# Moving a skipped overflow block behind the last expert, with twelve constant matmuls in its old place

## The chip, the cores and the metric

The kernel runs on one core of one Trainium2 chip. The metric is device time in microseconds (us), from one execution of the whole program; the kernel before has a median of 1113.36 us over 3 runs (1112.92 to 1116.15).

## The reference

One residual layer over 1024 tokens of width 1024, all in float32, and a last norm. The mixer (a gated recurrence and a softmax attention) comes first and is not touched by the change. Then comes a mixture of experts in two levels:

```python
pg = softmax(t @ w_group + b_group)            # 4 groups, top 1
e_logits = (t @ w_expert + b_expert)[group]    # 4 experts in it, top 2
gates = one_hot(expert_id, 16) * weights       # each token goes to 2 of 16 experts
for e in range(16):
    h = silu(t @ w_gate[e]) * (t @ w_up[e])    # 1024 -> 512
    y = y + gates[:, e:e+1] * (h @ w_down[e])  # 512 -> 1024
h = h + y
out = rms_norm(h, final_norm)                  # h * rsqrt(mean(h*h) + 1e-6) * gain
```

## The kernel before, in words

The kernel is one long, unrolled program, written with a planner that assigns semaphores and buffers. The planner gives each engine its own list of instructions. An instruction that is written later may be issued earlier if its inputs and its buffer are ready; what is written earlier goes first where both are ready. `tc.issue_after(ins)` puts what is written inside its block, on the engine of `ins`, behind `ins` in that engine's list; it adds no wait for other engines.

After the mixer, the function `back(i)` routes tile `i` of 128 tokens (there are eight): norm, transposes, the router's matmul (L819), the choice of group and experts on VectorE, and the rank of each token within its expert by a matmul with a triangular constant (L836). `enlist(i)` scatters the token numbers and gates into a list per expert in HBM (`list_d`). Tokens stand normed in `t_d` and as residual `h_d`, both in HBM.

When all tiles are routed, the experts are sorted by their number of tokens. Each place in that order has a fixed capacity (192, 160, 136 or 128 tokens). If an expert got more tokens than its place holds, the rest goes into blocks of 128 "overflow" rows. Their number, `tov`, is computed on the chip, and `tvi` and `ordi` (L912, L914) hold it and the order; `last_v` is the VectorE instruction that writes `ordi`.

Then follow, in the order written: the gather of expert 0's tokens (L925 and L930, GpSimd's indirect DMA), the definitions of the expert functions, and the load of `tov` into a register of all five engines (L1151) with the overflow block under `tc.If(tov > 0)` (L1152 to L1204). The block builds a list of overflow rows, loops over the overflow blocks, loads the weights of each block's expert into buffers `WT[3..5]` and adds the result to `h_d`. Behind it, `ready` and the copy of L1206 hold back the split of the weights and the load of the fourth weight matrix, and the loop over 16 experts begins.

The first expert and most others use `expert_t`: transposes of the gathered tokens (L1057), split of each weight matrix into two parts `wh` and `wl` (L1045 on ScalarE, L1047 on VectorE or GpSimd), and three matmuls for each product (L246 to L248, `mm3`). The last two experts use `expert`, with plain float32 matmuls (L989, L1001, L1009). Six weight buffers `WT` of 2 MB hold two experts' weights; a load is issued by SyncE when its buffer is free.

While expert 14 runs, `final_all` reads all rows of `h_d` back, norms them and writes them to the output. Expert 14's rows (`final_rows`, L1289) and expert 15's rows (`final`, L1256) are normed by themselves and overwrite their rows of the output by GpSimd's indirect DMA. Before the change, `final` keeps expert 15's finished rows in a tile `y0`.

Of the kernel before, what the change touches and what calls it, by code (L numbers as in the profile page):

```python
# [7 lines left out]
F32 = mybir.dt.float32  # L8
F32R = mybir.dt.float32r
I32 = mybir.dt.int32  # L10
U32 = mybir.dt.uint32
AF = mybir.ActivationFunctionType
OP = mybir.AluOpType
AX = mybir.AxisListType
# [3 lines left out]
D = 1024  # L18
S = 1024
NT = S // 128  # L20
KD = D // 128
E = 16
# [5 lines left out]
NOV = 16  # L28
NSLOT = E * CAP
NROW = NSLOT + NOV * 128  # L30
EPS = 1e-6
NU = 16
NWARM = 14
BIG = 1.0e30
NEG = 3.0e38
LEVELS = (1, 2, 4, 8, 16, 32, 64)
# [44 lines left out]
def build(ctx, tc, x, attn_norm, w_in, hg_lb_logits, hg_norm, fox_f_bias, fox_norm, w_out, ffn_norm,  # L81
          w_group, b_group, w_expert, b_expert, w_gate, w_up, w_down, final_norm, cf, ci, cl0, out, dbg=None):
    nc = tc.nc
# [16 lines left out]
    def cbank():  # L100
        return ps.tile([128, 512], F32, name="ch", tag="ch", bufs=NB["ch"])
# [26 lines left out]
    def C(k):  # L128
        o, n = offs[k]
        return cft[:, o:o + n] if o < nce else cfl[:, o - nce:o - nce + n]  # L130
# [53 lines left out]
    b = rbank()  # L184
# [555 lines left out]
    NW = 6  # L740
# [147 lines left out]
    b = bank()  # L888
# [26 lines left out]
    with tc.tile_pool(name="me", bufs=2, side="right", reuse_waits="tile") as me:  # L915
# [45 lines left out]
        with tc.issue_after(gathered[-1].ins):  # L961
            enlist(NT - 1)
        ready = [None, None]
        fnc = me.tile([1, 1], F32, name="fnc", bufs=1)

        def xprep(rows, xg):
# [13 lines left out]
        def expert(W, rows, xT, last=None, mid=None, res=None):  # L980
# [15 lines left out]
            if last:  # L996
                (m, idx, gt), = rows
                by = (cbank(), cbank())
                for q in range(4):
                    for c in range(2):  # L1000
                        T.matmul(by[c][0:m], hT[:, q, 0:m], wd[:, q, c * 512:c * 512 + 512], start=q == 0, stop=q == 3)  # L1001
                final(me.tile([m, D], F32, name="y0", bufs=1), m, idx, [z[0:m] for z in by], gt, last[0])
                return
            yT = me.tile([128, KD, WCAP], F32, name="yT", bufs=1)
            for k0, k1 in ((0, 3), (3, 6), (6, 8)):
# [142 lines left out]
                                              in_=yr, in_offset=None, compute_op=OP.add)  # L1148
                tc.declare_no_dep(p1.ins, p0.ins, reason="distinct rows")

        tov = nc.values_load(tvi, min_val=0, max_val=NOV)  # L1151
        with tc.If(tov > 0):  # L1152
            olist = dr.tile([NOV * 128, 2], F32, name="olist")
            G.dma_start(olist, cl0[NSLOT:NSLOT + NOV * 128])
            dg = me.tile([E, 2, E], F32, name="dg", bufs=1)
            V.tensor_scalar(dg[:, 0], e16, qc[:, 5:6], None, op0=OP.mult)
            V.tensor_scalar(dg[:, 1], e16, qc[:, 3:4], None, op0=OP.mult)
            b = cbank()
            T.matmul(b[:, 0:2 * E], ones[0:E, :], dg.rearrange("e a b -> e (a b)"), start=True, stop=True)
            ntl = me.tile([128, 4, E], F32, name="ntl", bufs=1)  # L1160
            V.tensor_copy(ntl[:, 0], b[:, 0:E])
            V.tensor_copy(ntl[:, 3], b[:, E:2 * E])
            lt2 = me.tile([128, E, E], F32, name="lt2", tag="sg")
            V.tensor_mul(lt2, C(C_LT).rearrange("p (a b) -> p a b", a=E), ntl[:, None, 0].to_broadcast([128, E, E]))
            V.tensor_reduce(ntl[:, 1], lt2, axis=AX.X, op=OP.add)
            V.tensor_add(ntl[:, 2], ntl[:, 1], ntl[:, 0])
            V.tensor_tensor(lt2, ntl[:, None, 2].to_broadcast([128, NOV, E]), C(C_JJ)[:, :, None].to_broadcast([128, NOV, E]), op=OP.is_le)
            oi = me.tile([128, NOV], F32, name="oi", bufs=1)
            V.tensor_reduce(oi, lt2, axis=AX.X, op=OP.add)
            V.tensor_scalar(oi, oi, float(E - 1), None, op0=OP.min)  # L1170
            oii = me.tile([128, NOV], I32, name="oii", bufs=1)
            V.tensor_copy(oii, oi)
            t1 = me.tile([128, 2 * NT, E], F32, name="t1", tag="sg")
            cp = me.tile([128, 2, NT], F32, name="cp", bufs=1)
            V.tensor_mul(t1, e1a.rearrange("p c i e -> p (c i) e"), ntl[:, 3:4].to_broadcast([128, 2 * NT, E]))
            V.tensor_reduce(cp.rearrange("p c i -> p (c i)"), t1, axis=AX.X, op=OP.add)
            V.tensor_mul(t1, e1a.rearrange("p c i e -> p (c i) e"), ntl[:, 1:2].to_broadcast([128, 2 * NT, E]))
            od = me.tile([128, 2, 2, NT], F32, name="od", bufs=1)
            V.tensor_reduce(od[:, 0].rearrange("p c i -> p (c i)"), t1, axis=AX.X, op=OP.add)
            V.tensor_sub(cp, rks, cp)  # L1180
            V.scalar_tensor_tensor(od[:, 0], od[:, 0], 128.0, cp, op0=OP.mult, op1=OP.add)
            V.tensor_scalar(od[:, 1], cp, 0.0, 1.0e6, op0=OP.is_lt, op1=OP.mult)
            V.tensor_add(od[:, 1], od[:, 1], od[:, 0])
            oix = me.tile([128, 2, NT], I32, name="oix", bufs=1)
            V.tensor_copy(oix, od[:, 1])
            for i in range(NT):
                for c in range(2):
                    G.indirect_dma_start(
                        out=olist, out_offset=bass.IndirectOffsetOnAxis(ap=oix[:, c, i:i + 1], axis=0),
                        in_=tg[:, c, i], in_offset=None, bounds_check=NOV * 128 - 1, oob_is_err=False)  # L1190
            with tc.For_i(0, tov) as j:
                ev = nc.values_load(oii[0:1, bass.ds(j, 1)], min_val=0, max_val=E - 1)
                lj = me.tile([128, 2], F32, name="lj")
                nc.sync.dma_start(lj, olist[bass.ds(j * 128, 128), :])
                li = me.tile([128, 1], I32, name="li")
                V.tensor_copy(li, lj[:, 0:1])
                W = []
                for q, w_ in enumerate((w_gate, w_up, w_down)):
                    src = w_[0, bass.ds(ev, 1)].rearrange("a (k p) c -> p (a k) c", p=128)
                    t = WT[3 + q].rearrange("p (k c) -> p k c", c=src.shape[2])  # L1200
                    nc.sync.dma_start(t, src)
                    W.append(t)
                rows = [(128, li, lj[:, 1:2])]
                expert(W, rows, xprep(rows, gather(rows)))  # L1204
        ready[:] = [None, last_v]
        G.tensor_copy(WT[3][0:1, 0:1], xg[0][0:1, 0:1])  # L1206
        wload(3)
# [95 lines left out]
        for e in range(E):  # L1303
            last = None
            if e == E - 1:
                last = held(e)
            nx = xg1 if e == 0 else gather(rows_of(e + 1), part_of(e + 1)) if e + 1 < E else None
            W = [loaded.get(3 * e + q) for q in range(3)]
            if e == 0:
                expert_t(W, rows_of(e), xg, part=part_of(e), pre=pre)  # L1310
            else:
                ft = final_all() if e == E - 2 else None
                if e < E - 2 and (part_of(e) or len(rows_of(e)) == 1):
                    expert_t(W, rows_of(e), xg, part_of(e))
                else:
                    xT = xT if last else xprep(rows_of(e), xg)
                    xT = expert(W, rows_of(e), xT, last, ft, held(e) if ft else None)
            xg = nx
            for q in range(3):
                if 3 * e + NW + q < 3 * E:  # L1320
                    wload(3 * e + NW + q)
    we_cm.__exit__(None, None, None)
    ps_cm.__exit__(None, None, None)
    ho_cm.__exit__(None, None, None)
# [23 lines left out]
```

## Time and profile before

| | |
|---|---|
| median of 3 runs | 1113.36 us |
| profiled execution, whole | 1111.55 us |
| its span, first to last instruction | 1109.7 us |
| TensorE busy | 1044.7 us (94%) |
| VectorE, ScalarE, GpSimd busy | 672.3, 489.2, 363.3 us |
| mean granted TensorE clock | 0.971 of full speed |

The profile is of one execution. PE is the matmul side of TensorE and PEld its weight loads; DVE is VectorE, ACT ScalarE, POOL GpSimd, SP SyncE. A name with q is the engine's queue, whose waits, branches and loads into registers are not counted as busy. PEclk is the clock that was granted to TensorE; it has two levels, 0.50 (1.2 GHz) and 1.00 (2.4 GHz). The routing ends and the first expert begins between 700 and 722 us; the experts run until about 1095 us.

### The profile page before, as it was taken

How to read it: one execution, taken by the hardware profiler on the slowest of the kernel's cores; microseconds unless marked ns; L12 is line 12 of the kernel's file. 1: busy time of each engine (PE TensorE's matmuls, PEld its weight loads, DVE VectorE, ACT ScalarE, POOL GpSimd, SP SyncE). 2: the span in 40 equal slices, each digit the busy share in tenths (PEclk: the TensorE clock that was granted, in tenths of full speed). 3: DMA queues.
4: the chain of work that ended last, by engine and by line, in shares of the span. 5: the costliest groups of instructions: out<-in, count | busy, mean ns of one | idle time of the engine just before them, and what ended most of it. 6: DMA issues, size and time to landing. Idle time of an engine off the chain costs nothing. (4 is left out here: it accounts for less than half of the span.)

```text
span 1109.7 us, 19260 instructions
## 1 busy us (share of the span) xinstructions
PE 1044.7 (94%) x7471; PEld 886.3 (80%) x7471; DVE 672.3 (61%) x1600; ACT 489.2 (44%) x845; POOL 363.3 (33%) x283
## 2 busy tenths in 40 slices
PE   7999999999999998899989899699999999999994
PEld 6989878778989887789867788576877778878793
DVE  5436445663596338825564676666778778777445
ACT  6423232422444233414442233465666767667341
POOL 2024113221141114300321233354655556545312
PEclk8999999999999999999989999699999999999997
DMA  7120521224111521163316952369999999999974
GB/s 244 40 58 21 158 62 38 67 49 105 39 46 32 135 64 30 59 185 128 99 54 216 385 165 76 126 221 373 370 332 319 362 320 376 301 321 373 290 294 168
DMA packets 103007, 197.12 MB, mean 178 GB/s; under 512 B 9660, under 2 KB 43564, under 8 KB 102912
## 3 DMA queue, kind: packets, MB, share of 16 engines
q1 hardware_dynamic: 91616, 173.12, 45.0%
q0 software_dynamic: 7568, 20.96, 7.6%
q10 hardware_dynamic: 3728, 1.77, 0.6%
q8 instruction: 60, 0.98, 0.4%
q14 instruction: 35, 0.29, 0.1%
HBM read 155.85 MB, written 30.68 MB: 168 GB/s over the span
## 5 line engine op out<-in xcount | busy, mean ns | idle before, releaser
L246 PE MATMUL bk<-whi,xhi 128*128 128x256 f32 (+1 forms) x384 | 112.6, 293 | 4.0 <-ACT whi L176 2.0
L1047 DVE TENSOR_TENSOR wl<-we,wh 128x1024 fp32r<-128x1024 f32 x64 | 91.8, 1445 | 34.7 <-ACT wh L1045 33.9
L248 PE MATMUL bk<-whi,xlo 128*128 128x256 f32 (+1 forms) x384 | 111.4, 290 | 0.2 <-DVE xlo L213 0.2
L247 PE MATMUL bk<-wlo,xhi 128*128 128x256 f32 (+1 forms) x384 | 110.4, 288 | 1.1 <-DVE wlo L177 1.1
L247 PE MATMUL ch<-wl,xh 128*128 128x512 f32 (+1 forms) x336 | 108.7, 324 | 0.0
L1045 ACT CAST wh<-wm 128x1024 fp32r<-128x1024 f32 x84 | 87.2, 1049 | 48.3 <-PE ch L248 47.6
L248 PE MATMUL ch<-wh,xl 128*128 128x512 f32 (+1 forms) x336 | 107.7, 322 | 0.0
L246 PE MATMUL ch<-wh,xh 128*128 128x512 f32 (+1 forms) x336 | 107.7, 327 | 0.0
L246 PE MATMUL bk<-xhi,whi 128*128 128x512 f32 x256 | 104.0, 406 | 1.7 <-DVE kl L299 1.4
L1045 ACT CAST wh<-we 128x1024 fp32r<-128x1024 f32 x84 | 87.2, 1049 | 39.8 <-PE ch L248 39.6
L1047 DVE TENSOR_TENSOR wl<-wm,wh 128x1024 fp32r<-128x1024 f32 x63 | 93.1, 1507 | 17.1 <-ACT wh L1045 17.1
L248 PE MATMUL bk<-xhi,wlo 128*128 128x512 f32 x256 | 103.1, 403 | 0.0
L247 PE MATMUL bk<-xlo,whi 128*128 128x512 f32 x256 | 102.5, 400 | 0.0
L246 PEld LDWEIGHTS bk<-whi,xhi 128*128 128x128 f32 x384 | 73.8, 192 | 5.8 <-ACT whi L176 2.3
L387 ACT ACTIVATE Lg<-Lg,mn 128x128 f32<-128x128 f32 (+3 forms) x64 | 49.7, 777 | 60.9 <-DVE mn L383 54.3
L247 PEld LDWEIGHTS bk<-wlo,xhi 128*128 128x128 f32 x384 | 74.1, 193 | 1.9 <-DVE wlo L177 1.6
L248 PEld LDWEIGHTS bk<-whi,xlo 128*128 128x128 f32 x384 | 74.1, 193 | 0.8 <-DVE xlo L213 0.4
L1047 POOL TENSOR_TENSOR wl<-we,wh 128x1024 fp32r<-128x1024 f32 x20 | 51.1, 2554 | 70.9 <-ACT wh L1045 70.9
L521 POOL TENSOR_TENSOR hK<-hK,hF 128x512 f32<-128x512 f32 x28 | 36.6, 1306 | 108.5 <-PE hc L503 100.5
L177 DVE TENSOR_TENSOR wlo<-wraw,whi 128x1024 fp32r<-128x1024 f32 (+1 forms) x26 | 33.3, 1279 | 63.8 <-ACT whi L176 63.8
L247 PEld LDWEIGHTS ch<-wl,xh 128*128 128x128 f32 x336 | 64.3, 191 | 9.1 <-issue 4.1
L405 ACT CAST ph<-ch 128x512 fp32r<-128x512 f32 (+1 forms) x80 | 43.0, 542 | 64.5 <-PE ch L400 62.4
(419 smaller groups left out, 2645.8 us busy)
## 6 DMA issues: line engine op xcount, KB each, us to landing
we<-in_w_gate_dram SPq DMA_DIRECT2D x8, 2048.0 KB, 19.8
we<-in_w_up_dram SPq DMA_DIRECT2D x8, 2048.0 KB, 18.3
we<-in_w_down_dram SPq DMA_DIRECT2D x8, 2048.0 KB, 18.0
wm<-in_w_gate_dram SPq DMA_DIRECT2D x8, 2048.0 KB, 8.4
wm<-in_w_up_dram SPq DMA_DIRECT2D x8, 2048.0 KB, 13.5
wm<-in_w_down_dram SPq DMA_DIRECT2D x8, 2048.0 KB, 15.2
wraw<-in_w_in_dram SPq DMA_DIRECT2D x26, 512.0 KB, 3.9
xt<-in_x_dram SPq DMA_DIRECT2D x8, 512.0 KB, 13.8
```

The source lines that it names most:

```text
L177: V.tensor_sub(lo, raw, hi.bitcast(F32))
L246: T.matmul(o, l[0], r[0], start=first, stop=False)
L247: T.matmul(o, l[0], r[1], start=False, stop=False)
L248: T.matmul(o, l[1], r[0], start=False, stop=last)
L387: A.activation(L[:, :nb * 128], L[:, :nb * 128], AF.Exp, scale=-1.0, bias=prev, accum_out=fl[:, 0, i, hh:hh + 1])
L405: LF['act'] = A.copy(ph[:, :o], b[:, :o])
L521: G.tensor_mul(k2[:, :, 0], k2[:, :, 0], tb.to_broadcast([128, n, hs]))
L1045: A.copy(hi, src)
L1047: (G if j % 3 == 2 else V).tensor_sub(lo, src, hi.bitcast(F32))
```

## The change

Three edits. The `If` with the overflow block moves, with its body as it was, behind the loop over the experts. As the output's rows are then already written, its body first writes expert 15's rows into `h_d` (they were only kept on the chip) and, at its end, runs `final_all` again. `final` keeps those rows in weight buffer `WT[3]` instead of `y0`, and `yl` remembers them. The load of `tov` into the registers stands behind expert 1. Where the `If` stood, twelve float32 matmuls of a constant with itself (`ones`, 128x128) write a PSUM bank that nothing reads.

```diff
+NGAP = 12
...
+        yl = []
...
-                final(me.tile([m, D], F32, name="y0", bufs=1), m, idx, [z[0:m] for z in by], gt, last[0])
+                yl.append(WT[(3 * E - 3) % NW][0:m, 0:D])
+                final(yl[0], m, idx, [z[0:m] for z in by], gt, last[0])
...
-        tov = nc.values_load(tvi, min_val=0, max_val=NOV)
-        with tc.If(tov > 0):
-            olist = dr.tile([NOV * 128, 2], F32, name="olist")
...
+        b = cbank()
+        with tc.issue_after(last_v.ins):
+            for _ in range(NGAP):
+                T.matmul(b[:, 0:128], ones, ones, start=True, stop=True)
         ready[:] = [None, last_v]
         G.tensor_copy(WT[3][0:1, 0:1], xg[0][0:1, 0:1])
         wload(3)
...
         for e in range(E):
...
                     xT = expert(W, rows_of(e), xT, last, ft, held(e) if ft else None)
+                if e == 1:
+                    tov = nc.values_load(tvi, min_val=0, max_val=NOV)
             xg = nx
...
+        with tc.If(tov > 0):
+            (m, idx, _), = rows_of(E - 1)
+            G.indirect_dma_start(out=h_d, out_offset=bass.IndirectOffsetOnAxis(ap=idx, axis=0), in_=yl[0], in_offset=None)
+            olist = dr.tile([NOV * 128, 2], F32, name="olist")
...
+            fa = final_all()
+            next(fa)
+            next(fa)
```

## Rows read from the trace of the kernel before

**Rows 1.** The page: busy time of an engine, share, instructions.

```profile
PE 1044.7 (94%) x7471; PEld 886.3 (80%) x7471; DVE 672.3 (61%) x1600; ACT 489.2 (44%) x845; POOL 363.3 (33%) x283
```

**Rows 2.** Windows: start:end, length, busy by engine (instructions), clock, DMA, GB/s.

```profile
700.00:750.00 50.00, 39.37 (x275) 31.03 (x275) 31.49 (x93) 27.11 (x36) 22.97 (x18) 0.80 0.56 190
750.00:800.00 50.00, 49.59 (x276) 36.29 (x275) 34.80 (x37) 30.71 (x38) 24.75 (x15) 1.00 1.05 369
...
1000.00:1050.00 50.00, 49.59 (x366) 38.98 (x359) 32.20 (x35) 27.34 (x35) 25.76 (x15) 1.00 0.98 336
```

**Rows 3.** Waits, 730 to 1060 us: total us, times, longest; largest of TensorE.

```profile
PEld ch L246 <- issue: 4.9, 10, 0.8
```

**Rows 4.** Windows of 4 us from routing to the first expert.

```profile
702.00:706.00 4.00, 1.71 (x8) 1.58 (x8) 2.61 (x19) 2.84 (x6) 1.99 (x2) 0.50 0.36 134
...
718.00:722.00 4.00, 4.00 (x13) 3.23 (x12) 1.38 (x2) 1.33 (x3) 0.00 (x0) 0.50 0.73 231
722.00:726.00 4.00, 4.00 (x19) 3.06 (x17) 2.93 (x5) 2.85 (x4) 0.27 (x1) 0.98 0.79 301
```

**Rows 5.** Timeline, 700 to 722 us: start, length, instruction, idle time before it.

```profile
701.48 1.72 PE L819 MATMUL ch<-wrt,tT 128*128 128x24 f32 x8
...
705.49 3.88 ACT L1045 CAST wh<-we 128x1024 fp32r<-128x1024 f32 x4 [0.19 <-issue]
705.49 0.61 PE L836 MATMUL ch<-mem,cfl 128*128 128x16 f32 x2 [2.29 <-DVE mem L833]
...
709.71 1.00 POOL L925 DMA_INDIRECT xg<-t_d,i  x1 [5.42 <-DVE qc L904]
...
710.20 0.21 PE L910 MATMUL bk<-perm,cfl 16*1 16x16 f32 x2
...
711.02 1.67 POOL L930 DMA_INDIRECT xgr<-t_d,ri  x1 [0.30 <-DVE ordi L914]
...
716.39 1.94 PE L1057 MATMUL bk<-cft,xg 128*128 128x128 f32 x8 [5.99 <-PEq L1152]
...
717.56 0.18 POOL L1206 COPY wm<-xg 1x1 f32<-1x1 f32 x1 [2.23 <-PE bk L1057]
```

**Rows 6.** Source view of L1152: ns min/median/max, first and last start; who waited.

```profile
L1152 POOLq EVENT_SEMAPHORE  x5: 17/43/4052, 712.2 to 716.5; - x5
...
L1152 PEldq COMPARE_BRANCH  x1: 4707/4707/4707, 711.2 to 711.2; - x1
...
L1152 POOLq COMPARE_BRANCH  x1: 57/57/57, 711.7 to 711.7; - x1
L1152 POOLq INC_SWDGE_SEM  x1: 736/736/736, 716.6 to 716.6; - x1
...
  PE bk L1057: 6.0, 1
```

**Rows 7.** Source view of L1151, the load of `tov`, on TensorE's queue.

```profile
L1151 PEldq TENSOR_LOAD <-tvi x1: 492/492/492, 710.6 to 710.6; - x1
```

**Rows 8.** DMA view, 700 to 730 us: what, queue, count, us from issue to landing.

```profile
xg<-t_d,i POOLq DMA_INDIRECT x1, 4.4
xgr<-t_d,ri POOLq DMA_INDIRECT x1, 4.8
```

**Rows 9.** Timeline of TensorE: passes of 128x128 at the start and near the end.

```profile
1.08 5.43 PE L186 MATMUL rb<-warm 128*128 128x128 f32 x28 [1.08 <-DVE br_bc L217]
...
1079.07 8.65 PE L989 MATMUL ch<-xT,wm 128*128 128x128 f32 x76
```

**Rows 10.** Timeline of the end: the last instructions of ScalarE and GpSimd.

```profile
1097.65 0.72 ACT L1254 ACTIVATE we<-we,qz 128x512 f32<-128x512 f32 x1 [0.29 <-DVE qz L1253]
...
1101.24 1.00 POOL L1256 DMA_INDIRECT out_dram<-we,la  x1 [2.19 <-DMA out_dram<-we,la]
```

**Rows 11.** DMA view, 1070 to 1110 us: the scatters into the output.

```profile
out_dram<-we,la POOLq DMA_INDIRECT x3, 3.2
```

**Rows 12.** Source view of L1344, the program's end, on GpSimd's queue.

```profile
L1344 POOLq DRAIN  x1: 7850/7850/7850, 1101.0 to 1101.0; - x1
```

More of the change, by code (lines that the diff above doesn't have):

```diff
@@ L1149, in expert_t @@
                 tc.declare_no_dep(p1.ins, p0.ins, reason="distinct rows")
-        tov = nc.values_load(tvi, min_val=0, max_val=NOV)
-        with tc.If(tov > 0):
-            olist = dr.tile([NOV * 128, 2], F32, name="olist")
[L1154 to L1204, printed above, removed]
```

51 lines of the change are left out of this document (added).

## The prediction, made before the changed kernel ran

> **What bounds the kernel now.** I read the page first: its engine table and the stages of 50 us [rows 1, 2]. TensorE is busy for 94% of the span, and from 750 to 1050 us for 49.6 of every 50 us. The longest wait of one TensorE instruction there is 0.8 us [rows 3]. So in the experts TensorE is the bound, and time lost before the first expert is handed on to the end almost one for one; nothing later can absorb it. The stage 700 to 750 is the exception: 39.37 us busy and a granted clock of 0.80 [rows 2]. I therefore cut that stage into 4 us pieces [rows 4]: from 702 to 722 us the clock stands at 0.50 (1.2 GHz). The timeline [rows 5] names the work: the router's last matmuls (L819) end at 703.2, TensorE then waits 2.3 us for VectorE's ranking of the tokens (L836), works in small pieces until L910 ends at 710.41, and the first transposes of expert 0 (L1057) start at 716.39. The source view of L1152, the `If`, says why [rows 6]: TensorE's branch takes 4707 ns, and TensorE's wait ahead of L1057, 6.0 us, is put down to it. Last I read the end, where the change puts the `If`.
>
> **Start of the first expert.** Removed from this place: the load of `tov` (0.49 us on TensorE's queue [rows 7]), the branch, and on GpSimd a chain that ends with L1206 at 717.56. What is late next is the gather of the 128 tokens: it starts at 709.71 [rows 5] and lands 4.4 us later [rows 8], at 714.1. With 0.2 us for the wait, the transposes could start at 714.3, that is 2.1 us earlier; zero if the gather lands late, and no more than 2.3. The part rows `xgr` (issued 711.02, landing in 4.8 us, so 715.8 [rows 5, 8]) are read after those eight transposes, which take 1.94 us [rows 5], so they hide. SyncE's load of the fourth weight matrix is held by L1206 and comes up to 2 us sooner; none of TensorE's waits in the experts is for a weight DMA [rows 3], so I count it as nothing. If that cover went, the weight would be late for expert 1 only.
>
> **The twelve matmuls.** The 14 calls of L186, the same form, are 28 passes, so these are 24 of 128x128. L186 takes 5.43 us for its 28, or 0.194 us each, at the program's start; L989 at full clock takes 8.65 us for 76, 0.114 us each [rows 9]. That is 4.65 us or 2.7 us of TensorE. The code puts them in a block queued behind `last_v`, but `last_v` is a VectorE instruction and that call orders only instructions of the same engine; the matmuls read only a constant. So nothing ties them to this place, and the planner may issue them as soon as TensorE has nothing else ready. Rows 5 show it doing that to others: ScalarE's casts of L1045, written behind the `If`, run at 705.49, before it. Two bounds follow. If they stand behind L910, they run from 710.45 to 715.1 and the transposes start at 715.15: 1.2 us gained instead of 2.1. If all 24 stand in the gap of 2.3 us before L836, they make the ranking, and so the gather, 2.35 us late and eat the whole gain. I take the first, because the idle stretch behind L910 is by far the longest in rows 5, and because anything put into the earlier gaps is done by then. If they are issued far earlier, between 650 and 700 us, they cost up to 2.7 us there, where TensorE has hardly any idle time either (94% over the span [rows 1]).
>
> **The clock.** Before, TensorE starts working without pause at 716.39 and runs at half clock until 722.2: 5.8 us [rows 4, 5]. If it works without pause from 710.45, the same delay ends at 716.25, so only 1.1 us of expert 0 runs at half clock instead of 5.8, and half the difference is saved: 2.35 us. The other bound is zero: passes in the early gaps leave the stretch from 710 on as idle as it was. Between the bounds I take 1.8 us, nearer the full gain but short of it, because with a fast TensorE the first products come sooner to where they need the casts and differences that ScalarE and VectorE make of the transposes.
>
> **The load of `tov` behind expert 1.** TensorE's queue takes 0.49 us for it [rows 7], now in a stretch where TensorE is the bound, but the array has queued matmuls to work on. Between 0 and 0.5 us; I take 0.2. On the other engines the idle time hides it.
>
> **The `If` at the end.** TensorE has finished and ScalarE ends at 1098.37 (L1254) before the last scatter (L1256) is out [rows 10], so their branches, TensorE's 4.7 us included, hide behind it. GpSimd issues that scatter at 1101.24, it lands 3.2 us later at 1104.44, and GpSimd's drain, 7.85 us from 1101.02, ends at 1108.87 [rows 10 to 12]; the program ends 0.8 us after that. With the `If` skipped, GpSimd must first do what it did at L1152 [rows 6]: waits on its transfers (one took 4.05 us, until a scatter had landed) and the 0.74 us semaphore instruction. So the drain is reached at about 1105.3 instead of 1101.02. If its 7.85 us are a wait for something that ends at 1108.87 anyway, the cost is nothing; if they start over, it ends at 1113.15 and costs 4.3 us; if the drain has little left to do after so long a wait, up to 3.4 us are gained. The drain spans the scatter [rows 10, 12], so I take the waiting reading with most of the semaphore instruction on top: 0.5 us. The second body of normalisation in the `If` isn't executed when `tov` is zero; that it is zero here I read from the timeline, where no instruction of the body appears (after L1152's branch comes L1057).
> A rule of the Trainium skill speaks against this place. The trace shows a branch of 4.7 us on TensorE and of 0.06 us on GpSimd [rows 6]. Runtime: NRT & Kernel Launch, section "Instruction fetch mechanics", says that a taken branch to code outside the pages already held has to fetch it before going on. By that rule GpSimd, whose own branch was short, could have to fetch too behind the longer body; what that would give is the last rival.
> The destination `yl` in the fourth weight buffer instead of `y0` changes no wait: expert 15's matmuls that read that buffer (L989) end at 1087.7 [rows 9], and the down products that `final` needs come only behind them. Price nothing.
>
> **Sum.** 1.2 + 1.8 gained, 0.2 + 0.5 lost: 2.3 us faster. Against the profiled execution (span 1109.7, whole 1111.55) that is 1109.25. The median of the runs, 1113.36, is 1.8 us above the profiled execution; carried over, the forecast is 1111.1.
>
> **Rivals.**
> 1. *The matmuls are hoisted into the early gaps.* The free order speaks for it, and the planner's habit in rows 5; against it that the gaps are short. Gain 2.1 us at the start, less about 1.0 us of delay to the ranking, 0.4 us from the ramp, 0.7 lost behind as above: 0.8 us faster, 1112.6. Far earlier, in the 650 to 700 us stage, it is about the same.
> 2. *Everything is recovered.* Full ramp (2.35), start at 714.3 since fewer passes than 24 stand behind L910 (2.1), the end and `tov` free: 4.45 us, 1108.9. For it: TensorE hands time on one for one [rows 2]. Against it: more passes in the gap help the ramp and delay the start, so the two gains pull against each other.
> 3. *GpSimd's drain starts over* (the other side). It lies at the very end, where nothing covers it; price 4.3 us for the 0.5 in the sum, so 1.5 us slower than before: 1114.9. It decides once the drain takes more than 6.4 us from where it is reached (1105.3 to 1111.7, 2.8 us late, which is the whole gain). For it: the 7.85 us row; against it: the drain was issued before the scatter ran, so at least 3.4 us of it were waiting.
> 4. *The `If` moves, and the planner's whole list with it.* The order of expert 0 and 1 is redrawn; the six windows from 750 to 1050 (49.59 to 49.62 of 50 us, first and last in rows 2) leave 2.4 us of idle TensorE to win, and more to lose. Either sign: 2.4 us better or worse than the forecast, 1108.7 to 1113.5.
> 5. *GpSimd's branch is a long one too.* From 1101.0, with the 4.71 us of TensorE's branch [rows 6], it ends at 1105.7, and with the semaphore instruction the drain is reached at 1106.5, 1.2 us later than counted: 1112.3. For it: TensorE's row; against it: GpSimd's own row of 0.06 us at the same `If`. (The fetch that the Trainium skill describes on the page named above would be such a branch.)
>
> **How the numbers follow.** Forecast 0.36, first rival 0.25, second 0.15, third 0.12, fourth 0.06, fifth 0.06. A difference of 0.3% is 3.3 us, about what a measurement of this kernel can tell from no change; so faster means under 1110.0 and slower over 1116.7. Faster gets the second rival (0.14), a third of the forecast's own spread (0.13) and half of the fourth (0.03): 0.30. Slower gets the third where the matmuls are hoisted as well, 1116.4, or delay the ranking in full (0.05), the losing half of the fourth should it lose more than could be won (0.03), and all passes ahead of L836 with some loss behind (0.02): 0.10. The other 0.60 is no change that can be told. The range runs from full recovery with a drain that gains 1.5 of the 3.4 us, 1107.5, to just short of a drain that starts over with hoisted matmuls, 1116.0; the forecast's own range is 1109.5 to 1112.6.
>
> **What would show it.** Start: L1057's first row less than 6 us behind L910, and its wait no longer on L1152 but on the gather's DMA or nothing. Matmuls: where their 24 passes stand in TensorE's timeline, and whether L836 moved against L819. Clock: the granted clock of the 4 us behind the first transposes, above 0.50. End: the time from L1256 to the end of GpSimd's drain (7.6 us before). The forecast is wrong if the passes stand before L836, if the clock rises no sooner after L1057 than 5.8 us, or if the drain grows by more than 1 us.

## The result, and the profile after

The changed kernel takes 1126.40 us in the median of 6 runs (1121.75 to 1131.41), the kernel before 1113.68 beside it: ratio 1.0116, 95% interval [1.0085, 1.0147], or 12.9 us slower [9.5, 16.4]. The forecast was 1111.1, its range ended at 1116.0: wrong in sign and out of range. The profiled execution of after takes 1125.83 us, its span is 1123.7, 14.0 us over before's.

Where the router ends differs by up to 6.5 us from one profiled execution to the next (702.5 to 709.0 us), also between kernels whose code is the same up to there. So I measure from the end of its last matmul (L819 before, L820 after) to TensorE's last matmul, and from there to the end of the span. After: 400.1 + 21.0 us; before: 391.4 + 15.1. So 8.7 us are lost at the start of the experts and 5.9 behind the last one; the router ended 0.7 earlier in this execution.

**The start.** The windows of after that answer to [rows 2, 4] (start:end, length, busy of TensorE, its weight loads, VectorE, ScalarE, GpSimd, then clock, DMA share, GB/s):

```profile
700.00:750.00 50.00, 36.11 (x233) 29.39 (x234) 24.44 (x86) 20.51 (x28) 20.94 (x16) 0.76 0.41 134
750.00:800.00 50.00, 50.00 (x302) 36.03 (x301) 34.27 (x37) 29.69 (x36) 25.50 (x15) 1.00 1.05 370
```

```profile
710.00:714.00 4.00, 4.00 (x28) 3.64 (x28) 0.59 (x4) 0.00 (x0) 0.41 (x1) 0.75 0.46 131
714.00:718.00 4.00, 1.32 (x8) 0.69 (x6) 4.00 (x4) 1.07 (x2) 4.00 (x1) 1.00 0.00 0
718.00:722.00 4.00, 0.00 (x0) 0.00 (x0) 1.53 (x3) 0.00 (x0) 3.23 (x4) 0.60 0.60 152
722.00:726.00 4.00, 0.54 (x3) 0.55 (x4) 0.00 (x0) 0.00 (x0) 0.14 (x1) 0.50 1.02 371
726.00:730.00 4.00, 4.00 (x13) 3.15 (x13) 1.03 (x1) 1.18 (x2) 0.00 (x0) 0.62 0.12 43
```

From 750 on TensorE is as busy as ever; from 718 to 726 it does next to nothing, and the clock, up at 714, is down again. The timeline of after, beside [rows 5], tells why:

```profile
707.54 0.58 PE L943 MATMUL ch<-x,r 32*128 32x1 f32 x2 [0.21 <-DVE r L940]
708.05 4.13 PE L1157 MATMUL ch<-cfl 128*128 128x128 f32 x18
708.93 1.00 POOL L926 DMA_INDIRECT xg<-t_d,i  x1 [5.01 <-DVE ov L908]
712.11 0.38 PE L943 MATMUL ch<-x,r 32*128 32x1 f32 x2
712.42 0.94 PE L1157 MATMUL ch<-cfl 128*128 128x128 f32 x6
712.52 0.16 DVE L945 SCALAR_TENSOR_TENSOR ri<-ch,cfl 128x1 int32<-128x1 f32 x1 [3.44 <-PE ch L943]
713.49 1.09 PE L1060 MATMUL bk<-cft,xg 128*128 128x128 f32 x8
713.59 4.79 POOL L1159 COPY wm<-xg 1x1 f32<-1x1 f32 x1 [3.66 <-PE bk L911]
713.72 4.61 DVE L1050 TENSOR_TENSOR wl<-we,wh 128x1024 fp32r<-128x1024 f32 x4
715.16 0.40 PE L248 MATMUL ch<-wl,xh 128*128 128x512 f32 x1
718.53 0.99 POOL L931 DMA_INDIRECT xgr<-t_d,ri  x1 [0.15 <-DVE wl L1050]
725.46 0.69 PE L1078 MATMUL bk<-cft,xgr 128*128 128x128 f32 x2 [9.90 <-DMA xgr<-t_d,ri]
725.80 0.78 PE L249 MATMUL ch<-wh,xl 128*128 128x512 f32 x1
```

Read it from the top. Eighteen of the 24 passes of the twelve matmuls (L1157) stand between the two matmuls that compute the indices of the part rows (L943), the other six behind the second. So `ri` (L945) is computed 10.0 us after the router's end instead of 6.2. On GpSimd's list the 1x1 marker copy (L1159) now comes ahead of the gather of `xgr` (L931). That copy took 0.18 us before [rows 5]; here it takes 4.79. It began 0.13 us ahead of four subtractions of VectorE (L1050) and ended as they did, at 718.4. The gather goes out 16.0 us after the router's end instead of 7.8, and TensorE, whose list has the transposes of `xgr` (L1078) ahead of product 3, waits 9.90 us. In the kernel before the same four subtractions stood in two pairs:

```profile
710.62 2.36 DVE L1047 TENSOR_TENSOR wl<-we,wh 128x1024 fp32r<-128x1024 f32 x2
713.24 2.36 DVE L1047 TENSOR_TENSOR wl<-we,wh 128x1024 fp32r<-128x1024 f32 x2 [0.26 <-DVEq L1152]
```

The `If` of L1152 was what cut them, and the gather beside them took 1.67 us [rows 5]. It ended at 712.69, ahead of the first pair's end at 712.98, so it had not waited for the pair. That the cut made it short is not shown; e5 below has the same gather beside an uncut run.

**The end**, beside [rows 6, 10, 12], in three views of after: the timeline, then the source views of the `If` (L1277) and of the program's end (L1357):

```profile
1110.25 1.00 POOL L1209 DMA_INDIRECT out_dram<-we,la  x1 [3.17 <-DMA out_dram<-we,la]
```

```profile
L1277 POOLq EVENT_SEMAPHORE  x5: 17/43/43, 1110.8 to 1114.3; - x5
...
L1277 PEldq COMPARE_BRANCH  x1: 3892/3892/3892, 1097.9 to 1097.9; - x1
...
L1277 POOLq COMPARE_BRANCH  x1: 57/57/57, 1110.6 to 1110.6; - x1
L1277 POOLq INC_SWDGE_SEM  x1: 1796/1796/1796, 1114.4 to 1114.4; - x1
```

```profile
L1357 POOLq DRAIN  x3: 46/103/6607, 1116.2 to 1123.4; - x3
```

GpSimd skips the block in 0.06 us, passes its last wait at 1114.3, when the scatter has landed, runs a semaphore instruction of 1.80 us, and only then begins a drain of 6.61 us. Before, the drain of 7.85 us began 0.2 us ahead of the scatter and lay over it [rows 10, 12]. From the last scatter's start to the end of the span: 13.4 us, before 8.5. The scatter itself starts 7.6 us behind TensorE's last matmul instead of 6.7.

### The profile page after: what moved, and what is told of

It is laid out like the page before. It is cut to its first block, busy times and chain, and to the rows that moved or that the text cites. A ratio compares the mean times of both kernels' runs of the same rounds, so it can differ in the third digit from the quotient of the medians.

```text
span 1123.7 us, 19301 instructions
## 1 busy us (share of the span) xinstructions
PE 1049.5 (93%) x7495; PEld 890.0 (79%) x7495; DVE 671.2 (60%) x1600; ACT 488.1 (43%) x844; POOL 365.8 (33%) x283
## 5 line engine op out<-in xcount | busy, mean ns | idle before, releaser
L1050 DVE TENSOR_TENSOR wl<-we,wh 128x1024 fp32r<-128x1024 f32 x64 | 91.6, 1442 | 40.7 <-ACT wh L1048 39.9
L1050 DVE TENSOR_TENSOR wl<-wm,wh 128x1024 fp32r<-128x1024 f32 x63 | 92.8, 1503 | 17.5 <-ACT wh L1048 17.5
L1050 POOL TENSOR_TENSOR wl<-we,wh 128x1024 fp32r<-128x1024 f32 x20 | 51.0, 2549 | 75.2 <-ACT wh L1048 64.9
## 6 DMA issues: line engine op xcount, KB each, us to landing
wm<-in_w_up_dram SPq DMA_DIRECT2D x8, 2048.0 KB, 13.6
```

The costliest lines, as they stand in the source:

```text
L1050: (G if j % 3 == 2 else V).tensor_sub(lo, src, hi.bitcast(F32))
```

## The experiments

Theory A at the outset: the matmuls between the L943 pair and the marker copy ahead of the gather cost the start, and they alone. It became: VectorE and GpSimd hold each other off there, in both directions, and the matmuls choose which instruction is hit. Rivals: the planner's list, redrawn by the block at the end; something else that bounds the first products. For the end: GpSimd's drain that starts over, against the planner's list.

All runs in one table. The first columns are of the one profiled execution, in us behind the router's end: issue of the `xgr` gather, product 3, 24 and 48, TensorE's last matmul; then from there to the end of the span. A product here is a single matmul of `mm3`, counted from the first expert's first, and its start is given. The last column is what was timed against before in the same runs: ratio minus 1, times before's median. The run is VectorE's four subtractions of L1050, one ahead leaves one of them in its place, and l is the copy of the expert lists.

| kernel | gather | 3 | 24 | 48 | last | to end | us against before, 95% |
|---|---|---|---|---|---|---|---|
| before | 7.8 | 16.2 | 22.3 | 27.6 | 391.4 | 15.1 | |
| after | 16.0 | 23.3 | 29.7 | 35.9 | 400.1 | 21.0 | +12.9 [9.5, 16.4] |
| e17 (after again) | 16.0 | 23.2 | 29.5 | 35.8 | 399.9 | 21.0 | +13.6 [9.9, 17.4] |
| e1 no matmuls | 7.8 | 16.1 | 22.1 | 31.4 | 395.7 | 21.0 | +6.2 [3.5, 8.9] |
| e2 gather first | 10.4 | 16.4 | 22.7 | 33.2 | 397.1 | 21.1 | +8.9 [6.1, 11.6] |
| e3 matmuls behind | 7.8 | 18.7 | 24.4 | 31.2 | 395.1 | 21.1 | +8.9 [5.9, 12.0] |
| e4 no If | 11.5 | 16.9 | 23.4 | 31.9 | 395.7 | 15.1 | +8.4 [3.8, 12.8] |
| e5 before, with matmuls | 7.8 | 23.4 | 30.1 | 33.1 | 402.4 | 13.5 | +9.7 [6.8, 12.7] |
| e8 no matmuls, no If | 7.8 | 16.0 | 22.9 | 28.2 | 392.0 | 15.1 | +2.3 [-0.1, 4.8] |
| e9 e8, run behind xl | 7.8 | 15.8 | 20.6 | 28.1 | 390.7 | 15.1 | +3.1 [0.7, 5.6] |
| e12 e8, one ahead | 7.8 | 14.0 | 19.9 | 29.8 | 395.1 | 14.5 | +3.8 [1.3, 6.2] |
| e13 e1, one ahead | 7.8 | 13.7 | 19.9 | 28.4 | 393.8 | 20.1 | +9.2 [6.2, 12.4] |
| e14 e3, one ahead | 7.8 | 15.0 | 21.8 | 26.0 | 389.9 | 21.0 | +5.9 [2.9, 8.8] |
| e16 e13, l on GpSimd | 7.8 | 13.8 | 19.9 | 25.2 | 388.9 | 21.9 | +4.5 [2.1, 6.9] |
| e18 e12, l on GpSimd | 7.8 | 13.9 | 19.9 | 25.2 | 389.0 | 16.0 | -0.7 [-2.9, 1.6] |
| e10 before, second If | 7.8 | 16.2 | 21.3 | 26.6 | 390.4 | 15.1 | +1.7 [-0.8, 4.2] |
| e11 with one GpSimd DMA | 7.8 | 16.2 | 22.3 | 29.0 | 392.8 | 16.2 | +1.2 [-1.4, 3.8] |
| e15 with eight | 7.8 | 16.1 | 21.1 | 26.4 | 390.2 | 19.3 | +5.3 [2.9, 7.8] |

"To end" holds two things. From the last scatter's start to the end of the span it is 8.4 to 8.5 us in every kernel that has no GpSimd DMA in a block at the end, and 13.0 to 13.4 in every kernel with the overflow block there. The scatter's own start varies, from 5.0 us (e5) to 8.6 us (e16) behind TensorE's last matmul. "Last" does not repeat either: e10, e11 and e15 have before's start and read 390.2 to 392.8, and a kernel's single executions lie 10 us and more apart. Small differences are therefore read from the last column, and a difference of two of its entries is uncertain by about 4 us.

**e1_no_gap**: after without the twelve matmuls.

```diff
-        with tc.issue_after(last_v.ins):
-            for _ in range(NGAP):
-                T.matmul(b[:, 0:128], ones, ones, start=True, stop=True)
```

> The changed kernel without the twelve matmuls; all else as changed. Theory A (the twelve matmuls stand between the two matmuls of L943, so the index of the part rows is 3 us late, the marker copy goes ahead of their gather on GpSimd, and TensorE waits 9.9 us for the part rows): the wait of 9.9 us is gone, the first products follow the transposes within 3 us, TensorE's last matmul ends near 1093, the end keeps its 21 us from there, so about 1115 us, 11 us faster than the changed kernel and 1 to 2 us slower than before. Rival B (the loss comes from the If's leaving its place, whatever the matmuls do): the stall stays, 1126 us. Rival C (the matmuls cost their own time only): 4.7 us faster than changed, 1121.7 us.

1121.52 us: 6.7 less than after by the last column, half of the loss, where theory A had 1115. The gather goes out on time, yet it takes 5.03 us (714.15 to 719.18), again until just behind VectorE's run. That was not expected, and made me drop the first form of the theory.

**e2_gather_first**: the marker copy queued behind the gather, matmuls kept.

```diff
+        with tc.issue_after(gathered[-1].ins):
-        G.tensor_copy(WT[3][0:1, 0:1], xg[0][0:1, 0:1])
+            G.tensor_copy(WT[3][0:1, 0:1], xg[0][0:1, 0:1])
```

> The changed kernel with one order more: on GpSimd the marker copy into the fourth weight buffer is queued behind the gather of the part rows. The twelve matmuls stay where they are. Theory A: the gather starts near 713 instead of 718.5 and lands near 718, TensorE's wait shrinks from 9.9 to about 2.5 us, so about 7 us faster than changed, 1119 us. Rival B (If's leaving) and rival C (the matmuls' own time): no difference, 1126 us.

1124.12, where theory A had 1119: 4.0 us less than after by the last column, with intervals that overlap. The gather takes 0.97 us now, and the first scatter of the list behind it takes the blow:

```profile
718.30 4.61 DVE L1050 TENSOR_TENSOR wl<-we,wh 128x1024 fp32r<-128x1024 f32 x4
718.80 5.00 POOL L780 DMA_INDIRECT list_d<-tg,si  x1 [0.30 <-issue]
```

**e3_gap_behind**: the matmuls tied to TensorE's own L911.

```diff
-        with tc.issue_after(last_v.ins):
+        with tc.issue_after(last_p.ins):   # last_p: the matmul of L911
```

> The changed kernel with the twelve matmuls queued behind TensorE's own last matmul of the routing instead of behind a VectorE instruction. Theory A: the pair of L943 stays together, the gather of the part rows starts near 710.5 as before the change, no stall of 9.9 us; TensorE works from about 710 on, so its clock is at full speed some 5 us earlier than without them: about 1112.5 us, 2 to 3 us below the kernel without the matmuls. Rival B: 1126 us. Rival C: 1126 us, since the matmuls are all there.

1122.95, which none of the three had: not as bad as in their place, not good. The gather takes 5.03 us as in e1.

**e4_no_if**: after without the `tov` load and the block.

```diff
-                if e == 1:
-                    tov = nc.values_load(tvi, min_val=0, max_val=NOV)
-        with tc.If(tov > 0):
...
```

> The changed kernel without the overflow block and without the load of its count; the block is left out altogether. Theory D (GpSimd's drain counts 6.6 us from its last DMA instruction, and the skipped block puts waits and a semaphore instruction of 1.8 us ahead of it): everything up to the last scatter as in the changed kernel, with the stall of 9.9 us, and from that scatter's start to the drain's end 7.6 us instead of 12.6: about 1121 us. Rival E (the end is longer because the transfers land later, not because of the block): no difference, 1126 us.

The end is back at 15.1 us, so the block at the end owns those 5.9. The time, 1123.88, has the widest interval (5 runs) and doesn't decide between the two numbers expected. The start is not that of after, and the stall of 9.9 us did not come: the marker copy runs ahead of VectorE's run (0.18 us), the gather goes out at 11.5, and the scatter behind it is held for 4.35 us.

**e5_before_gap**: the kernel before, with the twelve matmuls behind its L910.

```diff
+        with tc.issue_after(last_p.ins):   # last_p: the matmul of L910
+            for _ in range(12):
+                T.matmul(b[:, 0:128], ones, ones, start=True, stop=True)
         tov = nc.values_load(tvi, min_val=0, max_val=NOV)
```

> The kernel before, block and If in the old place, with the twelve matmuls added behind the last rank matmul (its L910), ahead of the branch. If TensorE's 4.7 us branch runs while the passes stand in front of it, as the branch at the end of the kernel after does, the transposes stay at 716.4 and find the clock up: products 1 to 24 take 5.5 instead of 7.1 us, about 2 us gained, 1112 where before is 1114. If the branch waits for the passes, the start is 1 to 3 us later and the kernel is at 1114 to 1117.

1122.09, far over both numbers. The branch did run while the passes stood in front of it: the transposes start 13.2 us behind the router's end, as before. But the planner redrew ScalarE's list: the read of the expert lists (L1216), which must wait for GpSimd's scatters, now stands ahead of the branch and of the casts of the first transposes, and the passes bought nothing. From the timeline of e5, first the uncut run of subtractions with the gather and the scatter beside it, then ScalarE's list:

```profile
715.92 4.63 DVE L1047 TENSOR_TENSOR wl<-we,wh 128x1024 fp32r<-128x1024 f32 x4
716.33 1.67 POOL L930 DMA_INDIRECT xgr<-t_d,ri  x1 [0.30 <-DVE ordi L914]
718.30 2.02 POOL L779 DMA_INDIRECT list_d<-tg,si  x1 [0.30 <-DVE wl L1047]
724.62 0.34 ACTq L1216 DMA_DIRECT2D lr<-list_d  x1
725.78 1.11 PE L1057 MATMUL bk<-cft,xg 128*128 128x128 f32 x4 [3.33 <-ACTq L1156]
727.16 1.07 ACT L1059 CAST xh<-bk 128x512 fp32r<-128x512 f32 x2
```

**e8_no_gap_no_if**: the edits of e1 and of e4 together, both diffs as above.

> The kernel after without the twelve matmuls and without the tov load and the If (the overflow block is left out). Theory A: the two costs add. The end is back at 15.1 us from TensorE's end to the program's, and the start keeps its loss, since VectorE's four subtractions of L1050 still run without a break while GpSimd gathers: 1121.5 - 5.9 = 1115.6, one to two us above before, with a gather or scatter that takes 4 to 5 us. Theory B (the loss of the start comes from the block at the end, by the planner's list): no GpSimd transfer is long, and the time is before's or 4 us less.

1116.07, near the 1115.6 of theory A, in which the two costs add. By e1 against e8 the end costs 3.9 us, by after against e4 4.5 (two starts that differ), and by the later pairs e13 and e12, e16 and e18 5.4 and 5.2. By after against e1 the matmuls cost 6.7 us, by e4 against e8 6.1. What is left of the start without them, e8's 2.3 us, is not told from zero. The hold is there without any `If`:

```profile
715.02 4.61 DVE L1050 TENSOR_TENSOR wl<-we,wh 128x1024 fp32r<-128x1024 f32 x4
715.44 5.03 POOL L931 DMA_INDIRECT xgr<-t_d,ri  x1 [0.31 <-DVE ordi L915]
```

**e9_subs_behind_no_if**: e8, with VectorE's run of subtractions queued behind `xl`.

```diff
-                V.tensor_sub(xl[:, 4 * g:4 * g + 4], ...)
+                xs = V.tensor_sub(xl[:, 4 * g:4 * g + 4], ...)
+            if pre:
+                ready[1] = xs
```

> As e8_no_gap_no_if (the overflow block is left out), with VectorE's first four subtractions of L1050 queued behind the two xl of L1063, so that no long run of VectorE stands beside GpSimd's gathers and scatters of the list. Theory A (a GpSimd transfer that begins beside the run is held until the run ends): all four take 1.0 to 1.7 us, xgr lands 4 us earlier, the list is read before 720, products 25 to 48 don't wait; product 1 is some 1.2 us later than it could be, since its wl is made last. 3 us less than e8, about 1112. Theory C (the transfer's length has nothing to do with VectorE): the gather still takes 4 to 5 us, and the time is e8's or 1 us more.

That VectorE's run is what holds the gather is shown; with the run moved, the same gather takes a fifth of the time:

```profile
715.14 0.97 POOL L931 DMA_INDIRECT xgr<-t_d,ri  x1 [0.30 <-DVE ordi L915]
```

But the time, 1115.98, is e8's: the half of the expectation that matters for a tuner failed. Product 24 comes 2.3 us sooner, product 48 no sooner.

**e12_one_sub_ahead_no_if, e13_one_sub_ahead**: one subtraction stays ahead, three go behind `xl`; without and with the block at the end (e13 is e1 with this edit).

```diff
             for p in range(KD // 2):
+                if pre and p == 1:
+                    ready[1] = xs
```

> As e8_no_gap_no_if (the overflow block is left out, no twelve matmuls), with one of VectorE's four subtractions of L1050 left in its place and three queued behind the xl of L1063. Theory A (GpSimd's transfer is held until VectorE's run ends): the xgr gather takes at most 2.5 us, both scatters of the list 1.0, the list is read by 17 us less than 3 after the router's end, product 2 finds its wl, and TensorE's end comes 389 to 390 us after the router's (e8 392.0, before 391.4): 2 us under e8. Theory C (the first products are bound elsewhere): as e9, the gain is lost before the 48th product and the time is e8's.

> The kernel after without the twelve matmuls, with the If at the end, and with the subtractions of e12. If the late list is what made TensorE wait 0.4 and 0.9 us for lr and l in e1_no_gap and lost the clock there, these waits and the second low stretch of the clock go: TensorE's end 390 to 391.5 us after the router's end (e1: 395.7), the end keeps its 21 us: about 4 us under e1, 1117.5. If e1's loss comes from the planner's list with the block at the end, it stays at 1121.5.

1117.16 and 1122.62: no gain in either, though products 3 and 24 are 2 to 3 us earlier than in e8 and e1. TensorE's end, 395.1 and 393.8, is over the 389 to 390 and the 390 to 391.5 that the theory gave. Products 25 to 48 take 9.9 us in e12, before 5.3. The timeline there:

```profile
725.98 2.62 POOL L1050 TENSOR_TENSOR wl<-we,wh 128x1024 fp32r<-128x1024 f32 x1 [8.00 <-ACT wh L1048]
726.31 2.44 DVE L1175 COPY l<-lr 16x256 f32<-16x256 f32 x1
728.89 0.57 PE L1178 MATMUL ch<-perm,l 16*128 16x16 f32 x2 [1.74 <-DVE l L1176]
```

A copy of VectorE that takes 0.27 us in before begins 0.33 us behind a subtraction of GpSimd and ends 0.15 us behind it. TensorE waits 1.74 us for it, and the clock stands at 0.50 from 728.7 to 735.5. The same copy took 1.95 us in e1 and 2.31 in e4; in before it came 0.3 us ahead of GpSimd's subtraction.

**e16_list_copy_gpsimd, e18_list_copy_gpsimd_no_if**: that copy on GpSimd's own list, in e13 and in e12.

```diff
-            V.tensor_copy(l4[:, 0:2] ...)
-            V.tensor_copy(l4[:, 2] ...)
+            G.tensor_copy(l4[:, 0:2] ...)
+            G.tensor_copy(l4[:, 2] ...)
```

> As e13_one_sub_ahead (If at the end, no twelve matmuls, one subtraction ahead), with the two copies from lr to l on GpSimd instead of VectorE, ahead of GpSimd's subtraction on its own list. Theory A (VectorE and GpSimd hold each other off): the copies take under 1 us, TensorE doesn't wait 1.7 us for l, products 25 to 48 take 5 to 6 us instead of 8.5, TensorE's end 390 to 391.5 us after the router's (e13: 393.8): 2 to 3 us under e13, still 5 to 6 over before by the end. Theory C (the start is bound by something else): as e13.

> As e16 without the If and the tov load (the overflow block is left out), so that the end is that of before. Theory A: what the start gains when neither collision is there and TensorE has no branch: TensorE's end 388.5 to 390 us after the router's (before 391.4), 1 to 3 us faster than before. Theory C: as e12, 2 to 4 us slower than before.

1117.65 and 1113.38: 4.7 and 4.5 us less than e13 and e12 by the last column. Products 25 to 48 take 5.3 us in both. In e18:

```profile
726.19 1.17 POOL L1175 COPY l<-lr 16x256 f32<-16x256 f32 x1 [7.52 <-DMA lr<-list_d]
727.57 2.37 POOL L1050 TENSOR_TENSOR wl<-we,wh 128x1024 fp32r<-128x1024 f32 x1
727.81 0.39 PE L1178 MATMUL ch<-perm,l 16*128 16x16 f32 x2
```

With both collisions shortened (the gather still takes 1.63 us), the start that has no branch of 4.7 us ends at 389.0 instead of 391.4 in the profile; timed, e18 is not told from before. So this is no version that beats both kernels, all the less as it has no overflow block.

**e14_gap_and_one_sub**: the edits of e3 and of e13 together: the matmuls behind L911, one subtraction ahead.

> As e13 with the twelve matmuls, queued behind L911. If they do what the clock could give them (products 1 to 24 at the full clock), up to 2 us under e13. If they only stand in front of the transposes (e3: 11.5 us after the router's end, e1: 10.7), 0 to 1 us over e13; if they redraw the planner's list on ScalarE or GpSimd, more than that.

1120.65. Under e13 by 3.3 us, with intervals that overlap; not by the way expected: products 3 and 24 are later than e13's. There VectorE's copy came ahead of GpSimd's subtraction and took 0.28 us, and products 25 to 48 take 4.2 us.

**e10_end_if_too, e11_end_if_gpsimd, e15_end_if_eight**: the kernel before, with a second skipped `If` behind the last expert: around the repeated norm alone, then with one and with eight GpSimd DMAs in it.

```diff
+        tend = nc.values_load(tvi, min_val=0, max_val=NOV)
+        with tc.If(tend > 0):
+            for _ in range(8):               # e15; once in e11, not at all in e10
+                G.indirect_dma_start(out=h_d, ..., in_=gn_bc[0:m], in_offset=None)
+            fa = final_all()
+            next(fa)
+            next(fa)
```

> The kernel before with its block in the old place, and a second load of the count and a skipped If (around final_all alone) behind the last expert. Theory A: GpSimd passes the wait for its last scatter, the semaphore instruction of 1.8 us, and a drain that starts only then and lasts 6.6 us: TensorE's end to the program's end goes from 15.1 to 21.0 us, the start stays as it is, and the kernel is 5.9 us slower than before. Rival: the end of the kernel after is late because of its planner's list, not the If: then 15.1 and before's time.

> As e10_end_if_too (the kernel before with a second, skipped If behind the last expert, which cost about 1 us), with one indirect GpSimd DMA to h_d added in that block. Theory A2 (what costs at the end is a block with GpSimd DMAs: skipped, it still makes GpSimd wait until its last scatter has landed and then run a semaphore instruction, and the drain's 6.6 us count from there): TensorE's end to the program's end goes from 15.1 to 20 to 21 us, 5 to 6 us slower than e10. Rival (the length or the engines of the block of after do it): 15.1, and e10's time.

> As e11_end_if_gpsimd, with eight indirect GpSimd DMAs in the skipped block at the end instead of one; the block of the kernel after has over sixteen. Theory A3 (GpSimd's DMAs go round eight semaphores; leaving a skipped block moves on each one that the block would have used, and one whose transfer is still under way is waited for): GpSimd waits some 4 us until the last scatter has landed, then the semaphore instruction of 1.8 us and the drain's 6.6: TensorE's end to the program's end 20 to 21 us, about 5 us slower than e11 and 6 slower than before. Rival (the wait in the kernel after comes from its block's reads and writes): 16.2 us as e11.

e10 came out as its rival had it and refutes theory A in its first form: an `If` alone costs nothing there (15.1 us). It doesn't prove the rival, that the planner's list is to blame: in e11 and e15 the last scatter starts 6.6 us behind TensorE's last matmul as in before, and the end is late all the same. With one DMA the semaphore instruction appears and no wait (16.2, neither number of e11); with eight the wait for the landing as well (19.3, a little under the 20 to 21 expected; the rival had 16.2). The source views of e11, then e15:

```profile
L1323 POOLq COMPARE_BRANCH  x1: 53/53/53, 1107.2 to 1107.2; - x1
L1323 POOLq INC_SWDGE_SEM  x1: 1750/1750/1750, 1107.4 to 1107.4; - x1
```

```profile
L1323 POOLq EVENT_SEMAPHORE  x4: 17/43/2787, 1100.5 to 1103.5; - x4
L1323 POOLq COMPARE_BRANCH  x1: 53/53/53, 1100.4 to 1100.4; - x1
L1323 POOLq INC_SWDGE_SEM  x1: 1767/1767/1767, 1103.6 to 1103.6; - x1
```

**e17_after_again**: after, with an empty diff.

> The kernel after, unchanged. If its loss of 12.9 us is 5.9 at the end and the rest at the start (8.7 us between the router's end and TensorE's end in its profile), a second profile shows the marker copy of 4 to 5 us on GpSimd again, TensorE's wait of about 10 us for xgr again, and the time is 1124 to 1128. If the start was an accident of one execution, it is 1119 to 1121.

1126.77, and a second profile with the same start: a marker copy of 4.78 us, a wait of 9.77 us for `xgr`, 399.9 us to TensorE's last matmul.

## Why the prediction was wrong

**Start of the first expert: the failed step.** The transposes did start sooner: L1060 starts 11.0 us behind the router's end, before 13.2, a gain of 2.2 us where the sum has 1.2. What failed is the next step, that the part rows "are read after those eight transposes", "so they hide". It left the gather of `xgr` at its old place and length, and gave the marker copy (L1206 there) no new place in GpSimd's list. In after the copy goes first and lasts 4.79 us beside VectorE's run, the gather goes out 8.2 us later, and TensorE waits 9.90 us for it. That lost time is handed on came true: after is 8.3 us behind at the 48th product and 8.7 at TensorE's end. GpSimd's durations came from a trace in which the `If` stood at that place in VectorE's queue as well. In the five profiles that have it there the gather takes 1.58 to 1.67 us; in the three without it in which the gather begins beside the run of four (e1, e3, e8) it takes 5.03.

**How long the hold lasts.** In e5 the four subtractions run without a gap, and yet the gather and the scatter are let in after about one subtraction each: they end 2.6 and 0.2 us ahead of the run's end. Later in the profile of after a gather that begins beside a run of three ends 1.4 us ahead of the run's end:

```profile
807.39 4.28 DVE L1050 TENSOR_TENSOR wl<-wm,wh 128x1024 fp32r<-128x1024 f32 x3 [0.19 <-ACT wh L1048]
808.48 1.80 POOL L931 DMA_INDIRECT xgr<-t_d,ria  x1
```

So a hold over a whole run was seen at one place only, the run of four ahead of the first product in after and those of its variants that keep it. An uncut run is not enough for it, and what else it takes is open.

**The twelve matmuls.** Right that nothing ties them to their place. Wrong in where they go: not ahead of L836, and only six of the 24 passes near L910; eighteen stand between the halves of L943. I had bounded their cost at 2.35 us; it is 6.7 (after against e1) or 6.1 (e4 against e8), each uncertain by about 4 us. In the profile of after the way is that they delay `ri` and the planner puts the marker copy ahead of the gather.

**The clock.** It did come up sooner (1.00 from 714 to 718, before 0.50 until 722 [rows 4]) and was lost again in the wait of 9.90 us: 0.50 from 718.8 to 729.0 and from 735.9 to 739.3. The 1.8 us were not had. No experiment shows a gain by the passes: e3 is no faster than e1, and e14's advantage over e13 lies elsewhere.

**The load of `tov`.** Costs nothing that shows: SyncE runs it at 719.5, the other engines only near the end. TensorE's, 1.41 us from 1096.4, lies under its last matmuls.

**The `If` at the end: the second failed step.** I took 0.5 us, reading the drain as a wait for something that ends at its old time anyway; it is 5.9 in the profile (21.0 against 15.1). The third rival, given 0.12, had the mechanism: the drain starts over. Its 4.3 us were near the 4.9 between the scatter and the end, in part by luck: the semaphore instruction takes 1.80 us and not 0.74 and the landing 4.0 and not 3.2, while the drain that starts over takes 6.61 and not 7.85. The row that I weighed against it, 7.85 us begun ahead of the scatter [rows 12], was a drain that waits for the scatter's 1.0 us of issue and then lasts 6.6 us: 1102.2 to 1108.9. The remaining 1.0 us is the later scatter, which waits 3.17 us for the scatters of expert 14's rows to land instead of 2.19 [rows 10]. This wait is 2.68 to 3.20 us in every kernel with the overflow block at the end, and 2.19 to 2.20 in e4, e8, e9, e11, e12, e15 and e18, which don't have it there; how the block does it is open.

**The rivals.** The first, hoisting into early gaps, had the right suspicion and a small price. The fifth falls: GpSimd's branch takes 0.06 us and TensorE's 3.89 lies under its last matmuls. The fourth, the redrawn list, is real: e5 loses 8 us by the 24th product through it. e12 and e13 lose 2 us more behind the 72nd product than e8, which was not traced to its cause. The time of after doesn't need it beyond the marker copy.

**What the trace of before could have told.** The gather of 1.67 us beside the scatters of 1.0 in the same queue. The Trainium skill, SBUF — State Buffer, section "Who interferes with whom", says that a VectorE instruction with two SBUF inputs contends with a GpSimd instruction that reads SBUF, and that issue order decides which of the two blocks. The runs agree that there is blocking, in both directions (5.03 and 0.97 us in e8 and e9; 2.44 us in e12), but in after the copy lost although it had begun 0.13 us first. The same section infers that a `tensor_tensor` of VectorE, as these subtractions are, doesn't hold up the generation of DMA descriptors; here the indirect gathers and scatters were held, at which step isn't shown.

Open are the share of each collision in a single execution of after, and why GpSimd is let in after one subtraction in before and e5 and only at the run's end in e1.

## What to carry to other kernels

When something is removed from all queues, ask of each engine what closes up, and which engine it then meets; a duration read from the old neighbours holds only with them. A skipped block of several GpSimd DMAs costs a landing, a semaphore instruction and a whole drain when it is the last thing of the program. Filler work needs a dependence on its own engine, and even then the planner may redraw other lists, so look at each list, not at the filler.

## What the runs showed of the hardware

- A GpSimd instruction begun beside VectorE's 128x1024 subtractions is held. In before and e5 it is for about the one subtraction that runs: 1.67 us for a gather and 2.02 for a scatter, alone 0.97 to 1.0. In after, e1, e2, e3, e4, e8 and e17 it is until the end of the run of four: 4.79 us for a copy of one element (0.18 alone), 5.03 for a gather, 4.35 and 5.00 for a scatter. The copy ends 0.05 us behind the run, the DMAs 0.8 to 0.9.
- The other way round, a VectorE copy of 16x256 begun beside GpSimd's subtraction of 2.3 to 2.6 us takes 1.95 to 2.44 us (0.27 alone).
- GpSimd's drain at the program's end ends 6.6 us behind its last DMA or semaphore instruction of the DMA kind: before 1102.24 to 1108.87, after 1116.20 to 1122.81, e11 1109.17 to 1115.77.
- Leaving a skipped block at the program's end costs GpSimd a semaphore instruction of 1.75 to 1.80 us if the block holds a GpSimd DMA (e10, without one, has none), and with eight also a wait until its last transfers have landed.
- TensorE's branch past the overflow block takes from 0.45 us (e1, e16) to 4.81 us (e11, at the old place), past the short block of e10, e11 and e15 0.24 us; in after its 3.89 us lie wholly under matmuls issued ahead of it.
